# Modulation strips that fill whole quadrants, and a new order of the first chains, in a two-layer diffusion trunk

## The chip, the cores and the metric

The kernel runs on one core of one Trainium2 chip. The metric is the device time of one execution in microseconds, as the median of several runs.

## What is computed

Two layers of a diffusion trunk are applied to 1024 latent tokens and 128 context tokens of width 1024, in float32. Each layer begins with an adaptive modulation: for each of the two conditions, `c` for the latent tokens and `c_ctx` for the context tokens,

```
m = silu(cond) @ w_ada + b_ada            # (1024,) @ (1024, 3072)
shift, scale, gate = split(m, 3)
h = rms_norm(x, norm_g) * (1 + scale) + shift
```

In layer 0 `h @ w_in` feeds a convolution module (two 512-wide halves a and b, gated, a depthwise convolution of width 31, layer norm) and a neighbourhood attention; their outputs are gated, projected and added to x. Layer 1 is a pooling mixer with the same modulation. Products of h and weights are made in three parts: each float32 operand is split into a rounded high half and a low half, and high*high, high*low and low*high are added up in PSUM.

## The kernel before, in words

**Tokens and channels.** The nine token tiles of 128 rows (tile 8 is the context) form three groups of 384: group 0 has tiles 0 to 2, group 1 tiles 3 to 5, group 2 tiles 6 to 8. `norm_x` scales a tile by its rstd: a square with a sum on ScalarE, two small operations on GpSimd, a multiplication on VectorE. `h_chunk(g, ..., k)` makes chunk k (128 channels) of h for a group: three transposes on TensorE into a `tp` bank (there are two), shift and scale on ScalarE, a cast to the high half on VectorE, and the subtraction for the low half, on GpSimd for even k and on VectorE for odd k.

**Modulation of layer 0.** Shift and scale come in four parts m = 0 to 3, each for two chunks of h (2m and 2m + 1), from four loads of 512 KB (`load_wada(m)`). `ada0_rows(m)` is 32 matmuls on TensorE (64 instructions) whose stationary operand is `sc`, silu of the two conditions, two columns for each of eight k. The four strips of a part are put at PSUM partitions 0, 32, 64 and 96, two rows each. Four copies on VectorE (L333) move these rows into `ads`, which a memset has cleared. `ada0_cols(m)` turns `ads` by a transpose (L338) and adds bias and norm weight on VectorE (L273 to L279) to get `SH` and `SC`.

**Modulation of the rest** (gates of both layers, shift and scale of layer 1) is done later in the same manner, a step of 8 matmul instructions at a time between the main chains (`ada_strips`, L360). Two of its strips go through `ada_cols`: a memset of `adr` on GpSimd (L382), four copies on VectorE (L384), then `ada_turn` (L390) transposes.

**The first chains.** `first_chains` runs the first matmuls against w_in: column blocks x = 0 and 1 for group 0 and x = 0 for group 1, six accumulators in PSUM, chunk by chunk as h and weights arrive. `C(k, which)` issues six matmuls (two accumulators, three products) for each pair (x, g) in `which`; `T(k, g)` makes a chunk of h. The weights come in two halves: `split_w0(c, u)` splits the half u (chunks 4u to 4u + 3) of column block c into `whi` on ScalarE (L186) and `wlo` on VectorE (L187). Within `first_chains` TensorE, ScalarE and VectorE take their instructions in the order in which the code is written; GpSimd, SP, and everything after that is ordered by a scheduler. Tiles 6 and 7 are loaded into memory that holds part 3 of w_ada, so their load waits for `ada0_rows(3)`; tile 8 takes the place of tile 0.

**After that** the other column blocks follow on TensorE, while the depthwise convolution goes on beside them: some taps on ScalarE (L551) and GpSimd (L553), the others on VectorE (L564). The copies of `ada_cols` stand in VectorE's queue among those taps.

**Names in the profile.** `wada` is a part of w_ada of layer 0, `wad` a step of the rest, `tp`, `mm` and `cv` are PSUM banks, `whi`/`wlo` the halves of weights, `h` those of h.

Of the kernel before, what the change touches and what calls it, by code (L numbers as in the profile page):

```python
# [15 lines left out]
P = 128  # L16
# [3 lines left out]
G = 384  # L20
# [26 lines left out]
def _body(tc, nc, A, O, const, wp, arena, tmpp, smp, psp):  # L47
# [33 lines left out]
    make_identity(nc, ident)  # L81
    mhalf = const.tile([P, 16], F32, name="mhalf")
    gp.memset(mhalf, -0.5)
# [59 lines left out]
    ve.scalar_tensor_tensor(cu, th0, 1.0, V[:, :16], ALU.add, ALU.mult)  # L143
    sc = const.tile([P, 8, 2], F32, name="sc")
    ve.tensor_scalar(sc.rearrange("p k c -> p c k"), cu.rearrange("p (c k) -> p c k", c=2), 0.5, None, ALU.mult)

# [136 lines left out]
    ads = [const.tile([P, P], F32, name=f"ads{i}") for i in range(2)]  # L283
    for t in ads:
        gp.memset(t, 0.0)
    for t in range(3):
# [19 lines left out]
    raw0[0, 0] = load_raw0(0, 0)  # L306
    raw0[1, 0] = load_raw0(1, 0)
    for t in range(3, 6):
        load_x(t)
    load_wada(1)  # L310
    load_wada(2)
# [3 lines left out]
    for t in (6, 7):  # L315
        load_x(t)
    split_w0(0, 0)
    adb = {}

    def ada0_rows(m):  # L320

        b = adb[m] = bank("tp")
        for k in range(8):
            for x in range(2):
                for q in range(2):
                    r = 32 * (2 * x + q)
                    te.matmul(
                        b[r : r + 2, :P], sc[:, k, :], wt[m, k // 4, x][:, k % 4, q * P : (q + 1) * P],
                        start=(k == 0), stop=(k == 7), tile_position=(0, r),
                    )  # L330
        t = ads[m % 2]
        for r in range(0, P, 32):
            ve.tensor_copy(t[r : r + 2, :], b[r : r + 2, :P])  # L333

# [13 lines left out]
    def ada_strips(l, col, n, fin):  # L348
# [3 lines left out]
        def step(k):  # L352
# [5 lines left out]
            for q in range(4):  # L358
                r = 32 * q
                te.matmul(  # L360
                    st["b"][r : r + 2, :n], sc[:, k, :], w[:, q * n : (q + 1) * n],
                    start=(k == 0), stop=(k == 7), tile_position=(0, r),
                )
# [14 lines left out]
    def ada_cols(l, b, c0):  # L378

        t = slot(ADS[st_i[0] % len(ADS)], name="adr")[:, :G]  # L380
        st_i[0] += 1
        gp.memset(t[:98, :], 0.0)  # L382
        for r in range(0, P, 32):
            ve.tensor_copy(t[r : r + 2, :], b[r : r + 2, :G])  # L384
        return lambda: ada_turn(l, t, c0)
# [79 lines left out]
    def first_chains():  # L465
# [10 lines left out]
        def T(k, g):  # L476
            h_chunk(g, [xt[t] for t in range(3 * g, 3 * g + 3)], 0, h0, k, "tp")

        h0[0] = hslots(range(4))
        ada0_rows(0)  # L480
        ada0_cols(0)
        T(0, 0)
        T(1, 0)
        for k in range(2):
            C(k, ((0, 0),))
        split_w0(1, 0)
        for t in range(3, 6):
            norm_x(t)
        h0[1] = hslots(range(4, 8))
        for k in range(2):  # L490
            C(k, ((1, 0),))
        T(0, 1)
        T(1, 1)
        ada0_rows(1)
        for k in range(2):
            C(k, ((0, 1),))
        ada0_cols(1)
        for k in (2, 3):
            for g in range(2):
                T(k, g)  # L500
        for m in (2, 3):
            ada0_rows(m)
            C(2 * m - 2)
            ada0_cols(m)
            T(2 * m, 0)
            T(2 * m, 1)
            if m == 2:
                split_w0(0, 1)
            C(2 * m - 1, ((0, 0), (1, 0)))
            T(2 * m + 1, 0)  # L510
            T(2 * m + 1, 1)
            if m == 2:
                split_w0(1, 1)
            C(2 * m - 1, ((0, 1),))
        for x in bs:
# [958 lines left out]
```

## Time and profile before

| | |
|---|---|
| median of 3 runs | 974.99 us (974.53 to 975.31) |
| the profiled execution | 977.55 us, span 975.8 us |
| TensorE busy | 948.4 us, 97% of the span |
| VectorE, ScalarE, GpSimd busy | 601.9, 404.4, 369.8 us |
| mean granted TensorE clock | 0.996 |

Times in the profile count from the start of the span. A row of the timeline gives start, duration, engine, line, operation, output and inputs, and how many instructions are merged in it; in brackets stands the idle time ahead of it and the engine or transfer that ended it. PE is TensorE's matmul queue, PEld its weight loads. In rows that merge matmuls the duration holds the pipelined tail of the last one.

### The profile page before, as it was taken

The numbers are of one execution on the slowest core, as the hardware profiler recorded it, in microseconds if no ns is written. First come the engines' busy times: TensorE is split into PE (matmuls) and PEld (weight loads), VectorE is DVE, ScalarE is ACT, GpSimd is POOL, SyncE is SP. The second block draws the span as 40 slices with busy tenths as digits, with TensorE's granted clock in tenths as the row PEclk, the third lists the DMA queues.
The fourth block names the chain that finished last, engine by engine and source line by source line (L and its number), as shares of the span: only waits on it lengthen the run. The fifth ranks groups of instructions, "written<-read, shape, count | busy, mean of one in ns | idle before, by whom it ended". The sixth has DMA issues, their size and how long they took to land.

```text
span 975.8 us, 16659 instructions
## 1 busy us (share of the span) xinstructions
PE 948.4 (97%) x6388; PEld 866.3 (89%) x6388; DVE 601.9 (62%) x1243; ACT 404.4 (41%) x815; POOL 369.8 (38%) x485
## 2 busy tenths in 40 slices
PE   4999999899999999999999999999999999999998
PEld 2899888789999999987887888889999999998887
DVE  3658999989783444457778447666335554585332
ACT  4374676765411244238887223344222122231010
POOL 2354899889943201024456145430000000004231
PEclk9999999899999999999999999999999999999999
DMA  9946955525111111135335412251111111133211
GB/s 311 304 190 153 348 183 184 173 88 185 46 47 46 48 44 44 36 90 142 109 114 175 130 65 108 84 165 44 34 43 33 44 44 55 65 112 129 105 65 66
DMA packets 87531, 108.54 MB, mean 111 GB/s; under 512 B 10700, under 2 KB 73036, under 8 KB 87339
## 3 DMA queue, kind: packets, MB, share of 16 engines
q1 hardware_dynamic: 82539, 95.93, 30.9%
q0 software_dynamic: 2576, 9.18, 2.4%
q10 hardware_dynamic: 2336, 2.36, 0.7%
q8 instruction: 50, 0.82, 0.3%
q14 instruction: 30, 0.25, 0.1%
HBM read 94.64 MB, written 21.57 MB: 119 GB/s over the span
## 4 chain that ended last, share of the span: by engine, by line
PE 82%; POOL 5%; DVE 3%; DMA 3%; ACT 2%; issue 2%; SPq 1%; DVEq 0%; ACTq 0%; POOLq 0%
PE mm L230 33%; PE mm L237 15%; PE mm L1210 10%; PE mm L1203 10%; POOL zc L553 5%; PE cv L985 3%; PE tp L976 2%; PE mm L952 2%; PE mm L1373 2%; DVE cv L564 1%; DMA x<-in_x_sample 1%; DMA raw<-in_w_in 1%; PE tp L443 1%; SPq L212 1%; PE cv L230 1%
## 5 line engine op out<-in xcount | busy, mean ns | idle before, releaser
L230 PE MATMUL mm<-h,whi 128*128 128x384 f32 x1504 | 389.5, 339 | 1.0 <-POOL h L450 0.4
L230 PEld LDWEIGHTS mm<-h,whi 128*128 128x128 f32 x1504 | 271.6, 189 | 6.8 <-issue 2.0
L230 PE MATMUL mm<-h,wlo 128*128 128x384 f32 x752 | 252.8, 337 | 0.0
L553 POOL TENSOR_TENSOR zc<-zc,gr 128x384 f32<-128x384 f32 x138 | 148.5, 1078 | 32.7 <-ACT gr L551 24.5
L237 PE MATMUL mm<-whi,h 128*128 128x256 f32 x864 | 160.6, 287 | 0.0
L237 PEld LDWEIGHTS mm<-whi,h 128*128 128x128 f32 x864 | 137.4, 194 | 6.5 <-ACT vst L694 3.3
L230 PEld LDWEIGHTS mm<-h,wlo 128*128 128x128 f32 x752 | 141.9, 189 | 0.0
L237 PE MATMUL mm<-wlo,h 128*128 128x256 f32 x432 | 123.3, 285 | 0.0
L187 DVE TENSOR_TENSOR wlo<-raw,whi 128x1024 fp32r<-128x1024 f32 (+1 forms) x56 | 67.5, 1206 | 53.3 <-ACT whi L186 53.2
L564 DVE SCALAR_TENSOR_TENSOR cv<-u,convw,cv 128x384 f32<-128x384 f32 (+1 forms) x208 | 95.8, 514 | 1.3
L1210 PE MATMUL mm<-wrh,zs 128*128 128x512 f32 x288 | 92.4, 392 | 0.2 <-POOL wrh L1179 0.2
L1203 PE MATMUL mm<-whi,zs 128*128 128x512 f32 (+1 forms) x304 | 92.5, 379 | 0.0
L186 ACT CAST whi<-raw 128x1024 fp32r<-128x1024 f32 (+1 forms) x56 | 56.9, 1018 | 69.8 <-PE mm L230 25.9
L237 PEld LDWEIGHTS mm<-wlo,h 128*128 128x128 f32 x432 | 84.0, 194 | 0.0
L1217 POOL TENSOR_TENSOR y<-y,og 128x512 f32<-128x512 f32 x34 | 48.6, 1430 | 83.4 <-DVE og L1215 80.3
L551 ACT ACTIVATE gr<-u,convw 128x384 f32<-128x384 f32 (+2 forms) x128 | 64.3, 531 | 30.5 <-POOL zc L553 29.8
L970 POOL TENSOR_SCALAR p<-p,st 128x512 f32<-128x512 f32 x64 | 48.6, 773 | 47.6 <-DVE st L968 31.7
L1203 PEld LDWEIGHTS mm<-whi,zs 128*128 128x128 f32 x304 | 56.0, 188 | 10.6 <-ACT whi L186 0.2
L1210 PEld LDWEIGHTS mm<-wrh,zs 128*128 128x128 f32 x288 | 53.9, 188 | 11.8 <-POOL wrh L1179 0.6
L1215 DVE TENSOR_TENSOR og<-mm,gr 128x512 f32<-128x512 f32 x34 | 23.3, 687 | 59.3 <-PE mm L1210 35.0
L533 ACT ACTIVATE th<-mm 128x384 f32<-128x384 f32 x48 | 23.5, 489 | 81.7 <-PE mm L230 81.5
L1203 PE MATMUL mm<-wlo,zs 128*128 128x512 f32 (+1 forms) x152 | 57.2, 378 | 0.0
(215 smaller groups left out, 1393.2 us busy)
## 6 DMA issues: line engine op xcount, KB each, us to landing
raw<-in_w_in SPq DMA_DIRECT2D x28, 512.0 KB
wad<-in_w_ada SPq DMA_DIRECT2D x16, 768.0 KB
wada<-in_w_ada SPq DMA_DIRECT2D x16, 512.0 KB
raw<-in_w_in SPq DMA_DIRECT2D x32, 256.0 KB
raw<-in_w_out SPq DMA_DIRECT2D x16, 512.0 KB
y0scr<-y POOLq DMA_DIRECT2D x9, 512.0 KB, 3.2
y<-y0scr SPq DMA_DIRECT2D x9, 512.0 KB
x<-in_x_sample SPq DMA_DIRECT2D x8, 512.0 KB
```

What stands on the lines that cost most here:

```text
L186: se.copy(hi[:, :n], raw[:, :n])
L187: ve.tensor_tensor(lo[:, :n], raw[:, :n], f(hi[:, :n]), ALU.subtract)
L230: te.matmul(out, wsl(units, a, k, c0, P), hsl(hs, b, k, g), start=(k == 0 and i == 0), stop=(k == nk - 1 and i == 2))
L237: te.matmul(out, hsl(hs, p, k, g, a, P), wsl(units, q, k, 0, 256), start=(k == 0 and i == 0), stop=(k == 7 and i == 2))
L551: se.activation(pr[:, o : o + n], src, AF.Copy, scale=w)
L553: gp.tensor_tensor(z, z, pr, ALU.add)
L564: ve.scalar_tensor_tensor(zp if k == 30 else acc, src, convw[:, c, k : k + 1], zp if k == NPTS[c] else acc, ALU.mult, ALU.add)
L970: gp.tensor_scalar(ps[i][:, e, :], ps[i][:, e, :], st[:, 4 + e : 5 + e], 0.0, ALU.mult, ALU.add)
L985: te.matmul(ob[64 * e : 64 * e + 64, i * P : (i + 1) * P], vw[j0 + i][x][:, 64 * e : 64 * e + 64], pts[i][:, e, n * P : (n + 1) * P], star ...
L1203: te.matmul(b[:, c0 : c0 + n], zs[p][:, k, :], WL[k // 2][q][:, k % 2, c0 : c0 + n], start=(k == 0 and i == 0), stop=(k == 7 and i == 2))
L1210: te.matmul(b, zs[p][:, k, :], WR[q][k // 3][:, k % 3, :], start=(k == 0 and i == 0), stop=(k == 7 and i == 2))
L1217: gp.tensor_tensor(yv, yv, t, ALU.add)
```

## The change

`sc` becomes a tile of 48 columns, the 16 values in the order of k and zeros behind them, and each strip matmul takes 32 columns of it from column 2k on. A strip then fills all 32 partitions of its quadrant: the first two rows are the two conditions as before, the other thirty hold products that nobody reads. One copy takes the whole bank, and the memsets of `ads` and `adr` go. Part 1 of w_ada is loaded ahead of tiles 3 to 5. The body of `first_chains` is written in another order, and the first split of weights stands behind the first `ada0_cols`.

```
-    sc = const.tile([P, 8, 2], F32, name="sc")
-    ve.tensor_scalar(sc.rearrange("p k c -> p c k"), cu.rearrange("p (c k) -> p c k", c=2), 0.5, None, ALU.mult)
+    sc = const.tile([P, 48], F32, name="sc")
+    gp.memset(sc, 0.0)
+    ve.tensor_scalar(sc[:, :16].rearrange("p (k c) -> p c k", c=2), cu.rearrange("p (c k) -> p c k", c=2), 0.5, None, ALU.mult)
...
-    for t in ads:
-        gp.memset(t, 0.0)
...
+    load_wada(1)
     for t in range(3, 6):
         load_x(t)
-    load_wada(1)
...
-                        b[r : r + 2, :P], sc[:, k, :], wt[m, k // 4, x][:, k % 4, q * P : (q + 1) * P],
+                        b[r : r + 32, :P], sc[:, 2 * k : 2 * k + 32], wt[m, k // 4, x][:, k % 4, q * P : (q + 1) * P],
...
-        t = ads[m % 2]
-        for r in range(0, P, 32):
-            ve.tensor_copy(t[r : r + 2, :], b[r : r + 2, :P])
+        ve.tensor_copy(ads[m % 2], b[:, :P])
...
-                    st["b"][r : r + 2, :n], sc[:, k, :], w[:, q * n : (q + 1) * n],
+                    st["b"][r : r + 32, :n], sc[:, 2 * k : 2 * k + 32], w[:, q * n : (q + 1) * n],
...
-        gp.memset(t[:98, :], 0.0)
-        for r in range(0, P, 32):
-            ve.tensor_copy(t[r : r + 2, :], b[r : r + 2, :G])
+        ve.tensor_copy(t, b[:, :G])
```

The new body of `first_chains`, where `one` is the pairs (0, 0) and (1, 0), `two` the pair (0, 1); beside it, the old one is in the listing above:

```
        ada0_rows(0); ada0_cols(0); split_w0(0, 0)
        T(0, 0); T(1, 0)
        C(0, (0, 0)); C(1, (0, 0)); split_w0(1, 0); C(0, (1, 0)); C(1, (1, 0))
        ada0_rows(1); ada0_cols(1); T(2, 0); T(3, 0)
        norm_x(3); norm_x(4); norm_x(5)
        C(2, one); C(3, one); T(0, 1); T(1, 1)
        ada0_rows(2); C(0, two); ada0_cols(2); T(2, 1); T(3, 1); C(1, two)
        T(4, 0); T(4, 1); split_w0(0, 1); C(2, two)
        T(5, 0); T(5, 1); split_w0(1, 1); C(3, two); C(4, one)
        ada0_rows(3); C(4, two); ada0_cols(3); T(6, 0); T(6, 1)
        C(5, one); T(7, 0); T(7, 1); C(5, two)
```

(Some lines are joined here by semicolons, and loops over k are written out.)

On TensorE, the rows around part 1's turn, the transpose of `ads`, before: it follows matmuls of group 1's chunks 0 and 1 (the accumulators `cv`).

```order
L230 MATMUL cv_248<-h_344,wlo_232 128x384
L230 MATMUL cv_247<-h_344,whi_231 128x384
L230 MATMUL cv_247<-h_345,whi_231 128x384
L230 MATMUL cv_247<-h_344,wlo_232 128x384
L230 MATMUL cv_248<-h_344,whi_231 128x384
L230 MATMUL cv_248<-h_345,whi_231 128x384
L230 MATMUL cv_248<-h_344,wlo_232 128x384
L338 MATMUL tp_376<-ident,ads_146 128x98
L443 MATMUL tp_429<-ident,x_116 128x128
L443 MATMUL tp_429<-ident,x_118 128x128
```

The same place after, from the end of part 1's rows to the first matmul of chunk 2:

```order
L326 MATMUL tp_334<-wada_186,sc 32x128 x2
L326 MATMUL tp_334<-wada_189,sc 32x128 x2
L335 MATMUL tp_334<-ident,ads_147 128x98
L438 MATMUL tp_372<-ident,x_116 128x128
L438 MATMUL tp_372<-ident,x_118 128x128
L438 MATMUL tp_372<-ident,x_120 128x128
L438 MATMUL tp_380<-ident,x_116 128x128
L438 MATMUL tp_380<-ident,x_118 128x128
L438 MATMUL tp_380<-ident,x_120 128x128
L232 MATMUL mm_238<-h_244,whi_286 128x384
```

The twelve matmuls between the rows and the turn are gone from there; group 1's chunks come after part 2's rows.

On ScalarE, the squares of tiles 6 and 7 (`x_227` and `x_229` before) among the chunks 6 and 7 of h, before:

```order
L186 CAST whi_568<-raw_214 128x1024
L126 ACTIVATE gr_73,ss_757<-x_227 128x1024
L448 ACTIVATE h_641<-tp_637,SH_137,SC_139 128x384
L448 ACTIVATE h_649<-tp_645,SH_137,SC_139 128x384
L126 ACTIVATE gr_73,ss_763<-x_229 128x1024
L448 ACTIVATE h_669<-tp_665,SH_137,SC_139 128x384
L448 ACTIVATE h_677<-tp_673,SH_137,SC_139 128x384
```

and after, where the tiles are `x_226` and `x_228`:

```order
L188 CAST whi_558<-raw_213 128x1024
L443 ACTIVATE h_628<-tp_624,SH_138,SC_140 128x384
L443 ACTIVATE h_636<-tp_632,SH_138,SC_140 128x384
L126 ACTIVATE gr_73,ss_744<-x_226 128x1024
L126 ACTIVATE gr_73,ss_750<-x_228 128x1024
L443 ACTIVATE h_656<-tp_652,SH_138,SC_140 128x384
L443 ACTIVATE h_664<-tp_660,SH_138,SC_140 128x384
```

Both squares now stand between chunk 6 and chunk 7.

On VectorE, the copies of the first strip that goes through `ada_cols`, among taps of two convolution accumulators, before:

```order
L564 SCALAR_TENSOR_TENSOR cv_2084<-u_1169,convw,cv_2084 128x384
L384 COPY adr_1927<-tp_1519 2x384
L564 SCALAR_TENSOR_TENSOR cv_1893<-u_743,convw,cv_1893 128x256
L384 COPY adr_1927<-tp_1519 2x384 x3
L564 SCALAR_TENSOR_TENSOR cv_2084<-u_1169,convw,cv_2084 128x384
```

and after:

```order
L570 SCALAR_TENSOR_TENSOR cv_2067<-u_1156,convw,cv_2067 128x384
L570 SCALAR_TENSOR_TENSOR cv_1880<-u_730,convw,cv_1880 128x128
L379 COPY adr_1914<-tp_1506 128x384
L570 SCALAR_TENSOR_TENSOR cv_2067<-u_1156,convw,cv_2067 128x384
L570 SCALAR_TENSOR_TENSOR cv_1880<-u_730,convw,cv_1880 128x256
```

One tap of 384 columns that stood ahead of the copies, and the tap of 256 that stood between them, now stand behind the copy. On TensorE the place of that transpose among the matmuls is unchanged.

More of the change, by code (lines that the diff above doesn't have):

```diff
@@ L81, in _body @@
     make_identity(nc, ident)
-    mhalf = const.tile([P, 16], F32, name="mhalf")
+    mhalf = const.tile([P, 8], F32, name="mhalf")
     gp.memset(mhalf, -0.5)
@@ L316, in _body @@
         load_x(t)
-    split_w0(0, 0)
     adb = {}
@@ L477, in T @@
             h_chunk(g, [xt[t] for t in range(3 * g, 3 * g + 3)], 0, h0, k, "tp")
+        one, two = ((0, 0), (1, 0)), ((0, 1),)
         h0[0] = hslots(range(4))
@@ L481, in first_chains @@
         ada0_cols(0)
+        split_w0(0, 0)
         T(0, 0)
@@ L486, in first_chains @@
         split_w0(1, 0)
+        for k in range(2):
+            C(k, ((1, 0),))
+        ada0_rows(1)
+        ada0_cols(1)
+        T(2, 0)
+        T(3, 0)
         for t in range(3, 6):
@@ L489, in first_chains @@
         h0[1] = hslots(range(4, 8))
-        for k in range(2):
-            C(k, ((1, 0),))
+        C(2, one)
+        C(3, one)
         T(0, 1)
         T(1, 1)
[L494 to L514, printed above, removed]
+        ada0_rows(2)
+        C(0, two)
+        ada0_cols(2)
+        T(2, 1)
+        T(3, 1)
+        C(1, two)
+        T(4, 0)
+        T(4, 1)
+        split_w0(0, 1)
+        C(2, two)
+        T(5, 0)
+        T(5, 1)
+        split_w0(1, 1)
+        C(3, two)
+        C(4, one)
+        ada0_rows(3)
+        C(4, two)
+        ada0_cols(3)
+        T(6, 0)
+        T(6, 1)
+        C(5, one)
+        T(7, 0)
+        T(7, 1)
+        C(5, two)
         for x in bs:
```

## The prediction

> **What bounds the kernel now.** The page comes first, for the span and the busy shares.
>
> ```profile
> span 975.8 us, 16659 instructions
> PE 948.4 (97%) x6388; PEld 866.3 (89%) x6388; DVE 601.9 (62%) x1243; ACT 404.4 (41%) x815; POOL 369.8 (38%) x485
> ```
>
> TensorE is busy for 97%, so a change is worth what it does to TensorE's 27.4 us of idle time, and to the speed at which it runs. The view of windows, cut where TensorE's state changes, says where that time lies (columns: PE, weight loads, DVE, ACT, POOL, then the granted clock).
>
> ```profile
> 0.00:21.31 21.31, 7.49 (x73) 3.81 (x73) 6.66 (x16) 8.09 (x12) 5.58 (x44) 1.00 0.92 306
> 21.31:63.54 42.23, 40.85 (x386) 36.91 (x387) 27.58 (x60) 19.95 (x35) 16.30 (x28) 1.00 0.95 301
> 63.54:170.99 107.45, 107.45 (x729) 96.64 (x727) 96.26 (x193) 71.71 (x140) 82.44 (x80) 1.00 0.62 201
> 170.99:174.14 3.15, 0.00 (x1) 0.03 (x1) 3.06 (x7) 1.78 (x3) 2.96 (x3) 0.84 0.26 86
> 174.14:179.60 5.46, 5.46 (x26) 5.46 (x27) 5.43 (x18) 3.58 (x7) 5.04 (x5) 0.50 0.59 192
> ```
>
> The change touches three of these stretches. Before 21.31 TensorE idles 13.8 us for data. In the first chains (21.31 to 63.54) it idles 1.4 us. Then it never stops until 170.99, where it stands still for 3.15 us and afterwards gets half the clock for 5.46 us. The view of TensorE's waits names the two long ones:
>
> ```profile
> PE tp L327 <- DMA wada<-in_w_ada: 8.1, 3, 6.3
> PE tp L390 <- POOL zc L553: 3.2, 1, 3.2
> ```
>
> The first is the wait for the first part of w_ada, whose loads the change leaves in place. The second is ada_turn's transpose of the strip `adr`. GpSimd is named as releaser, but the vector queue shows who came last:
>
> ```profile
> 168.85 2.57 DVE L564 SCALAR_TENSOR_TENSOR cv<-u,convw,cv 128x128 f32<-128x128 f32 x6
> 171.33 0.54 DVE L384 COPY adr<-tp 2x384 f32<-2x384 f32 x1
> 171.80 0.47 DVE L564 SCALAR_TENSOR_TENSOR cv<-u,convw,cv 128x256 f32<-128x256 f32 x1
> 172.30 1.70 DVE L384 COPY adr<-tp 2x384 f32<-2x384 f32 x3
> 174.14 0.72 PE L390 MATMUL tp<-ident,adr 98*128 98x98 f32 x3 [3.15 <-POOL zc L553]
> ```
>
> The four copies stand in a saturated queue of convolution taps and end at 174.00; the transpose starts 0.14 later.
>
> **The copy of the strips (a gain at 171).** One copy of 128x384 replaces four of 2x384 and a memset. A copy's time goes with its columns, not with its rows: 384 columns on 2 partitions take 0.54, and the next fence has 128 columns on 2 partitions at 1.19 / 4 = 0.30 and 48 columns on 48 partitions at 0.21. So I take 0.54 for the new one and 0.30 for the 128 columns of part copies. By the order, the new copy also stands one 384-column tap (about 0.5) earlier, and the tap between the copies now stands behind it. On the old clock it would end at 171.33 - 0.5 + 0.54 = 171.4 instead of 174.00. TensorE arrives at 170.99 with unchanged work ahead of it, so the wait would be 0.4 + 0.14 = 0.5, if both queues shift alike. The order of the loads on SP for the next weight units changes too (one ahead of two table writes), which may move the vector queue by a microsecond either way; I take a wait of 1.0, with 0 and 3.15 as ends. Gain: 3.15 - 1.0 = 2.15. With the pause that short I let the clock stay up, which returns half of 5.46, 2.73.
>
> **The start of the first chains (a gain at 20).**
>
> ```profile
> 3.46 0.21 DVE L138 COPY V<-tp 128x48 f32<-128x48 f32 x1 [3.46 <-PE tp L137]
> 16.12 1.19 DVE L333 COPY ads<-tp 2x128 f32<-2x128 f32 x4 [4.83 <-PE tp L327]
> 17.34 1.23 DVE L187 TENSOR_TENSOR wlo<-raw,whi 128x1024 fp32r<-128x1024 f32 x1
> 17.45 0.40 PE L338 MATMUL tp<-ident,ads 98*128 98x98 f32 x1 [1.38 <-DVE ads L333]
> 18.59 0.16 DVE L273 TENSOR_TENSOR SH<-tp,V 128x4 f32<-128x4 f32 x1
> 19.82 0.36 DVE L449 CAST h<-h 128x384 fp32r<-128x384 f32 x1 [0.80 <-ACT h L448]
> 20.26 1.00 POOL L450 TENSOR_TENSOR h<-h,h 128x384 fp32r<-128x384 f32 x1 [9.76 <-DMA x<-in_x_sample]
> 21.31 0.69 PE L230 MATMUL mm<-h,whi 128*128 128x384 f32 x1 [0.39 <-POOL h L450]
> ```
>
> Today the shift waits for four copies and for the weight split (1.23) that stands ahead of it. After, one copy ends at 16.4, the transpose at 16.9, shift and scale at about 17.5; the split moves behind them and ends at 18.7, the cast at 19.05, GpSimd's low half at 20.1. The matmuls start 1.2 earlier. The memset of `sc` replaces two larger ones on GpSimd and is hidden by the load of the vectors.
>
> **The new order of the chains (a loss at 27 to 60).** Here the change takes cover away. The rows, by step:
>
> ```profile
> 21.31 6.56 PE mm L230 x23
> 28.96 1.93 PE L327 MATMUL tp<-wada,sc 128*2 128x128 f32 x64 [0.43 <-ACT h L448]
> 30.89 2.29 PE cv L230 x12
> 33.30 0.16 DVE L273 TENSOR_TENSOR SH<-tp,V 128x4 f32<-128x4 f32 x1 [1.01 <-PE tp L338]
> 34.97 1.00 POOL L450 TENSOR_TENSOR h<-h,h 128x384 fp32r<-128x384 f32 x1 [4.58 <-DVE h L449]
> 42.19 2.11 PE mm L230 x12
> 44.30 0.65 PE tp L443 x6
> ```
>
> Part 1: its rows now follow the first 24 matmuls (20.1 + 6.6 = 26.7) and end at 28.6. Today 12 matmuls (2.29) stand between these rows and the turn, and cover the copies. After, the turn follows at once: copy and transpose 0.5, then from the shift to GpSimd's low half 35.97 - 33.30 = 2.7, some 3.3 in all. TensorE has the turn, six transposes (0.65) and one matmul for that time, so it idles about 2.3. Loading part 1 earlier buys nothing here: today these rows wait for ScalarE (the 0.43 above), not for their load.
>
> ```profile
> 21.39 1.05 ACT L126 ACTIVATE gr<-x 128x1024 f32<-128x1024 f32 x1
> 26.86 0.75 DVE L128 TENSOR_SCALAR x<-x,rstd 128x1024 f32<-128x1024 f32 x1 [0.71 <-POOL rstd L114]
> 20.00:30.00 10.00, 8.94 (x70) 8.23 (x74) 5.88 (x9) 6.07 (x10) 5.40 (x8) 1.00 1.09 353
> ```
>
> Group 1's normalisation takes 27.61 - 21.39 = 6.2 from its first square and now starts behind part 1's h, at about 31.4, so it ends at 37.6. TensorE is through with chunks 2 and 3 of group 0 (24 matmuls, 4.2) at 36.2: another 1.0 idle. Its x also lands later, with part 1's 2.1 MB ahead of it: 6 us at 353 GB/s, so by 27.4 if it landed at 21.4 before, well ahead of 31.4. Against these two pauses goes about 1.0 of small waits that stand there today (0.43 is one of them).
>
> ```profile
> 41.26 0.34 PE tp L443 x3
> 47.82 1.22 DVE L187 TENSOR_TENSOR wlo<-raw,whi 128x1024 fp32r<-128x1024 f32 x1
> ```
>
> Chunk 4 needs the second halves of the weights. From its transposes to the end of the second split today's queue takes 49.04 - 41.26 = 7.8, and nothing needs that split until after part 3's rows. After, the second half is used ahead of those rows, behind twelve transposes, 18 matmuls and two more: 1.3 + 3.15 + 0.35 = 4.8. The gap of 3.0 shrinks since transposes wait for their banks too; I take 2.2.
>
> ```profile
> 45.93 1.93 PE L327 MATMUL tp<-wada,sc 128*2 128x128 f32 x64
> 52.58 1.06 ACT L126 ACTIVATE gr<-x 128x1024 f32<-128x1024 f32 x1 [5.68 <-DMA x<-in_x_sample]
> ```
>
> Tiles 6 and 7 load into slots of part 3, so they land 52.58 - 47.86 = 4.7 after its rows. Those rows come later by the moved chains, and by the order both squares now stand ahead of chunk 7's h on ScalarE. That h is ready 4.7 + 2 x 1.2 + 0.6 = 7.7 after the rows, cast and low half 0.4 to 1.7 later (the low half stands behind tile 6's scaling). TensorE needs it after 30 matmuls and twelve transposes, 5.3 + 1.3, and a turn, some 7.0. That is 1.1 idle for the cast and up to 2.4 for the low half, less the little that stands there today; I take 1.1.
>
> Sum of the chains: 2.3 + 1.0 - 1.0 + 2.2 + 1.1 = 5.6 later, less the 1.2 of the start: 4.4. Its ends are 2 (the pauses half as long) and 7 (the unshrunk gaps). Nothing later takes that up, as TensorE does not wait from 63.54 to 170.99, and the vector queue of taps starts behind the same chains.
>
> **Wider weights.** The strips' stationary operand has 32 columns instead of 2.
>
> ```profile
> L327 PEld LDWEIGHTS tp<-wada,sc 128*2 128x2 f32 x256 | 6.9, 91 | 11.7 <-issue 6.7 <-DMA wada<-in_w_ada 2.7 <-ACT h L448 1.2
> L985 PEld LDWEIGHTS cv<-pt,vw 128*64 128x64 f32 x384 | 20.7, 137 | 3.2 <-issue 2.3 <-ACT pt L1139 0.9
> 470.56 1.97 PE L985 MATMUL cv<-pt,vw 128*64 128x128 f32 x32
> ```
>
> From 2 to 64 columns a load grows by 46 ns, so 30 columns cost some 22 ns each, and 448 loads 10 us if all lay on the path. But L985 has the same 128 columns streaming, on two column tiles with 64 columns of weights each: 1.97 / 32 = 62 ns, 123 for a round of its two tiles. L327 needs 1.93 / 64 = 30 ns, 121 for a round of four tiles with 2 columns each. Four loads of 32 columns are as much as two of 64, so a round should take 121 to 123: 2 ns x 16 rounds x 4 parts are 0.13, and with the strips of the other parts 0.2. I take this, the nearest row. The Trainium skill's "TensorE: Matmul & The Clock Gate", section "LDWEIGHTS (loading the stationary operand)", has the time go as the columns over 1.2 GHz, which would make the sum about 11 us worse if nothing hid it; the trace agrees on the slope and shows it hidden.
>
> **The sum.** 4.4 + 0.2 - 2.15 - 2.73 = -0.3. The profiled execution took 977.55 for its span of 975.8; the median of the plain runs is 974.99, 2.56 less. So 977.25 for such an execution, and 974.7 for the median. What measurement can tell from no change is 0.2%, 1.95 us: faster ends at 973.0, slower begins at 976.9.
>
> **Rivals.** (1) The forecast: the loss in the chains and the gain at 171 cancel, 974.7, by themselves 973.0 to 976.9; chance 0.47. (2) The clock falls in the new pauses. In the window of the old wait the granted clock averages 0.84, so it was halved in the last 2 x 0.16 x 3.15 = 1.0, after some 2.1 of idling. The wait for the split weights (2.2 to 3.0) and part 1's pause (2.3, broken by transposes) reach that point. Each fall costs up to 2.73: 977.4 for one, 980.2 for both. For it: the only long pause of the trace ended so. Against: theirs are just at the bound and hold transposes. Chance 0.18. The Trainium skill's page "TensorE: Matmul & The Clock Gate", section "Part 1: The HAM clock gate (the \"warmup\" mystery)", asks for an idle window of about 3.4 us; by that rule these pauses keep the clock, and the trace shows the fall sooner. (3) The wait at 171 stays, because the taps fall further behind than TensorE; from a lag of 2 us more the clock falls again: 974.99 + 4.6 = 979.6; chance 0.10. (4) Weight loads lie on the path: 10 us more, 984.7; chance 0.03. (5) The pauses of the chains are half as long, the split weights and tile 7 arriving in time: 2.0 in place of 4.4, and no wait at 171: 974.99 + 2.0 + 0.2 - 3.15 - 2.73 = 971.3. For it: the vector engine sheds 12 part copies in this stretch. Against: each pause is a chain of rows and no queue. Chance 0.22.
>
> **Range and chances.** Faster 0.22, same 0.47, slower 0.18 + 0.10 + 0.03 = 0.31. The range runs from case 5 to case 3 with both ends' neighbours, 971.3 to 979.6, and leaves out case 4, the double fall of case 2, and tails.
>
> **What would show it.** In the profile after, TensorE's idle time between 20 and 68 should be near 7 us, with waits before the first matmul of chunk 2 (about 2), before a matmul on the second split's low half (about 2) and before chunk 7; the first chains should end near 68 in place of 63.5. The transposes of `adr` should wait 1 us or less, with the clock at 1.00 behind them. Strip rounds should keep 1.9 for 64 matmuls. I am wrong if the first chains end by 65 (the covers I missed), if the clock drops ahead of 60, or if the wait at `adr` is still over 2.

## The result, and the profile after

| | before | after |
|---|---|---|
| median of 4 runs each | 975.15 us (974.53 to 976.22) | 983.90 us (981.19 to 984.62) |
| ratio, 95% interval | | 1.0083 [1.0064, 1.0103] |
| the profiled execution, its span | 977.55, 975.8 | 981.19, 979.4 |

The kernel is slower by 8.75 us, outside the range that the prediction gave. The two profiled executions differ by only 3.6 us, since that of before lies 2.40 above its median and that of after 2.71 below its own: 3.64 + 2.40 + 2.71 = 8.75. So the profile shows where the loss sits, and the medians how large it usually is. Part of the reason shows in the trace of after: its first 24 matmuls take 4.2 us (19.89 to 24.07) where those of before take 6.4 (21.31 to 27.71), most of them at twice the duration. None of the other 19 profiled executions has its first matmuls at that speed. Not even that of f1 below has, whose code is the same up to the first transpose of `adr`; its part 3's strips begin 1.6 us later than in after. So this profile flatters the kernel after.

The page of after, its first lines:

```profile
span 979.4 us, 16631 instructions
PE 948.1 (97%) x6388; PEld 867.6 (89%) x6388; DVE 596.2 (61%) x1225; ACT 403.9 (41%) x815; POOL 370.6 (38%) x482
```

VectorE is busy for 5.7 us less than before, as the change meant, and TensorE as long as before; what grew is TensorE's idle time. The view of windows, cut at the events of before (first full matmul chain, first chains done, TensorE stops for `adr`; the second only roughly, since the order of the matmuls there is another):

```profile
0.00:19.89 19.89, 7.18 (x74) 4.63 (x74) 5.96 (x13) 8.25 (x12) 5.43 (x43) 1.00 0.93 291
19.89:69.41 49.52, 42.89 (x389) 38.11 (x390) 24.30 (x51) 19.94 (x34) 15.81 (x27) 0.93 0.86 278
69.41:175.96 106.55, 106.55 (x725) 97.06 (x724) 95.20 (x186) 69.51 (x136) 80.92 (x77) 1.00 0.62 199
175.96:182.00 6.04, 2.97 (x16) 2.97 (x16) 6.04 (x14) 3.80 (x7) 5.57 (x7) 0.72 0.37 99
```

The chains start 21.31 - 19.89 = 1.4 us earlier. They idle 49.52 - 42.89 = 6.6 us where they idled 1.4, at a clock of 0.93 instead of 1.00, and end at 69.41 instead of 63.54. From there TensorE runs without a stop to 175.96, and stops at `adr` as before. The waits by name that the change brought or kept:

```profile
PE tp L385 <- DVE adr L379: 3.1, 1, 3.1
PE mm L232 <- DVE wlo L189: 2.6, 2, 2.4
PE mm L232 <- DVE h L444: 1.4, 2, 0.7
PE mm L232 <- POOL h L445: 1.3, 2, 0.6
PE tp L335 <- DVE ads L330: 0.8, 2, 0.4
```

And TensorE's timeline at the places of which the prediction spoke:

```profile
26.44 0.30 PE L335 MATMUL tp<-ident,ads 98*128 98x98 f32 x1 [0.41 <-DVE ads L330]
...
28.41 0.45 PE L232 MATMUL mm<-h,whi 128*128 128x384 f32 x1 [0.74 <-DVE h L444]
...
29.49 0.45 PE L232 MATMUL mm<-h,whi 128*128 128x384 f32 x1 [0.64 <-POOL h L445]
...
35.53 1.96 PE L326 MATMUL tp<-wada,sc 128*32 128x128 f32 x64 [0.43 <-ACT h L443]
...
48.53 0.44 PE L232 MATMUL mm<-h,wlo 128*128 128x384 f32 x1 [2.36 <-DVE wlo L189]
...
49.86 3.11 PE L326 MATMUL tp<-wada,sc 128*32 128x128 f32 x64
...
60.57 0.26 PE L174 MATMUL tp<-ident,rows 54*128 54x54 f32 x1 [0.46 <-ACT h L443]
...
62.26 0.49 PE L232 MATMUL mm<-h,whi 128*128 128x384 f32 x1 [0.49 <-DVE h L445]
...
62.86 0.84 PE L232 MATMUL mm<-h,whi 128*128 128x384 f32 x2
...
65.74 0.60 PE L232 MATMUL mm<-h,whi 128*128 128x384 f32 x2
...
179.03 0.75 PE L385 MATMUL tp<-ident,adr 98*128 98x98 f32 x3 [3.07 <-DVE adr L379]
```

Two things stand there beside the pauses. Part 3's strips (49.86) take 3.11 us where the same 64 matmuls took 1.96 at 35.53: behind the wait ahead of them the granted clock was 0.58 on average (48.80 to 52.90). From 62.26 to 65.74 it was 0.54, and two matmuls take 0.84 where they took 0.51 before the waits of 0.46 and 0.49. And the strips of part 3 begin at 49.86, not at 45.93, with what hangs on them. ScalarE and VectorE of after, the square of tile 6, the split of the fourth half of weights of the next column blocks, the tap ahead of the copy of `adr`, and that copy:

```profile
57.62 1.06 ACT L126 ACTIVATE gr<-x 128x1024 f32<-128x1024 f32 x1 [1.48 <-DMA x<-in_x_sample]
...
104.32 1.05 ACT L188 CAST whi<-raw 128x1024 fp32r<-128x1024 f32 x1 [4.61 <-DMA raw<-in_w_in]
...
105.40 1.23 DVE L189 TENSOR_TENSOR wlo<-raw,whi 128x1024 fp32r<-128x1024 f32 x1 [3.30 <-ACT whi L188]
...
175.21 1.36 DVE L570 SCALAR_TENSOR_TENSOR cv<-u,convw,zc 128x384 f32<-128x384 f32 x1 [0.42 <-POOL zc L559]
...
178.43 0.55 DVE L379 COPY adr<-tp 128x384 f32<-128x384 f32 x1
```

Of before, the rows that answer to the split and to the tap (the square was at 52.58, the last copies at 172.30 + 1.70):

```profile
99.64 1.22 DVE L187 TENSOR_TENSOR wlo<-raw,whi 128x1024 fp32r<-128x1024 f32 x1 [0.95 <-ACT whi L186]
...
167.57 1.36 DVE L564 SCALAR_TENSOR_TENSOR cv<-u,convw,zc 128x384 f32<-128x384 f32 x1 [0.40 <-POOL zc L553]
```

The square is 5.0 us later, the split 5.8, and the tap, which in both kernels has just waited 0.4 for GpSimd (`zc` is the accumulator of GpSimd's taps), 7.64. From the tap to the end of the copying it is 178.98 - 175.21 = 3.77 us instead of 174.00 - 167.57 = 6.43, so the single copy and its earlier place are worth 2.66. TensorE arrives 4.97 later (175.96 for 170.99). VectorE is later than TensorE by 7.64 - 4.97 = 2.67 at the tap, the copy saves just that, and the wait at `adr` is what it was.

### The profile page after: what moved, and what is told of

Same layout as the page of the kernel before. It is cut to its first block, busy times and chain, and to the rows that moved or that the text cites. A ratio compares the mean times of both kernels' runs of the same rounds, so it can differ in the third digit from the quotient of the medians.

```text
span 979.4 us, 16631 instructions
## 1 busy us (share of the span) xinstructions
PE 948.1 (97%) x6388; PEld 867.6 (89%) x6388; DVE 596.2 (61%) x1225; ACT 403.9 (41%) x815; POOL 370.6 (38%) x482
## 3 DMA queue, kind: packets, MB, share of 16 engines
q10 hardware_dynamic: 2336, 2.36, 0.7%
## 4 chain that ended last, share of the span: by engine, by line
PE 80%; DVE 8%; DMA 5%; SPq 2%; issue 2%; ACT 2%; POOL 1%; DVEq 0%; ACTq 0%; POOLq 0%
PE mm L232 32%; PE mm L239 14%; PE mm L1216 10%; PE mm L1209 10%; DVE cv L570 5%; PE cv L991 3%; DMA wada<-in_w_ada 2%; PE tp L982 2%; PE mm L958 2%; PE mm L1379 2%; DMA raw<-in_w_in 1%; POOL zc L559 1%; SPq L214 1%; DVE wlo L189 1%; DMA raw<-in_w_out 1%
## 5 line engine op out<-in xcount | busy, mean ns | idle before, releaser
L559 POOL TENSOR_TENSOR zc<-zc,gr 128x384 f32<-128x384 f32 x138 | 150.8, 1094 | 31.9 <-ACT gr L557 23.3
L189 DVE TENSOR_TENSOR wlo<-raw,whi 128x1024 fp32r<-128x1024 f32 (+1 forms) x56 | 67.9, 1214 | 49.8 <-ACT whi L188 49.1
```

What stands on the lines that cost most here:

```text
L189: ve.tensor_tensor(lo[:, :n], raw[:, :n], f(hi[:, :n]), ALU.subtract)
L559: gp.tensor_tensor(z, z, pr, ALU.add)
```

## The experiments

Eighteen kernels, each timed beside the kernel before on the same chip. In the first four, theory A is that the new order of chains and loads makes the loss, B that the full quadrants do. In the next four, A is narrower (TensorE's pauses are the loss, each worth its length). Theory E, formed from those, is that part 3's strips come late, tile 6 is loaded behind them, and ScalarE and VectorE run late from there.

**e1_strips.** The kernel before with the full quadrants alone: `sc` of 48 columns, 32-column strips, one copy each, no memsets (and a constant, `mhalf`, of 8 columns for 16, as in after).

> The kernel before with the full-quadrant strips alone; loads, chains and the first split stay as they were. Theory A (the new order of the chains is the loss): the one copy ends 2.6 us earlier on the vector queue, the transpose of adr waits 1 us or less instead of 3.15, the clock stays up behind it (2.7 us), and the first matmuls start 0.9 us earlier: about 969.5, at most 972. Theory B (the wide strips are the loss, by weight loads or by the products that nobody reads): slower than before, up to the 983.9 of the whole change, and a round of 64 strip matmuls takes clearly more than 1.93 us.

976.29 us, ratio 1.0016 [1.0001, 1.003]. Neither theory holds: no gain, and no loss near 8 us. The wait at `adr` fell to 1.91, not to 1.

**e2_order.** The kernel before with the new loads, the new place of the first split and the new chains, strips and copies as they were.

> The kernel before with the new loads, the new place of the first split and the new order of the chains; strips of two rows with four copies. Theory A: as slow as the whole change or slower, 983 to 987, since the strips take nothing from the chains; the first chains end near 69 instead of 63.5 and the transpose of adr waits 3 us or more. Theory B: near 975, as before.

986.66 us, 1.0109 [1.0089, 1.0129]: the order makes the whole loss. With the full quadrants it is some 2.5 less (1.0109 to 1.0083), but the intervals overlap, so that they soften it is not shown. Its waits show by what:

```profile
PE tp L389 <- DVE adr L383: 4.9, 1, 4.9
PE tp L337 <- DVE ads L332: 2.9, 3, 1.4
PE mm L230 <- DVE wlo L187: 2.6, 2, 2.4
```

The three waits for `ads` are 2.9 us with four copies each and 0.8 with one (after, above): where a turn has no matmuls to cover it, these waits are 2 us shorter with the single copy.

**e3_turn.** The kernel before with one line more, `adq[17], adq[18] = adq[18], adq[17]`: the first `adr` transpose comes one strip step later.

> The kernel before, with the transpose of the first adr strip moved one step of the strips later (the first step of the next strip takes its place). If that wait costs what the trace of before says, 3.15 us of standing still and 2.7 us of halved clock, this takes 969.3. Rival: the pause only moves to another place or its clock is lost there: 975, no change.

972.79 us, 0.9988 [0.997, 1.0005]. Its profiled span is 970.7, which is 5.1 less than that of before (a wait of 3.15 and half a clock's 5.46 gone), but its median is only 1.9 less. The kernel before ran between 972.6 and 977.7 in these comparisons; the profiled execution, with 977.55, is at the upper end. The wait and the clock's fall as the profile had them were not there to be won in every run. Single executions also differ ahead of the edit: the split of e3 begins at 98.19, 1.45 earlier than that of before, though the edit acts only at 171.

**e4_strips_split.** e1 with the first split behind part 0's turn, as in after.

> As e1, with the first split of weights written behind part 0's turn too. By the working of the prediction the first full matmul then starts 1.2 us earlier than before, of which the copies alone give a part; the time is 0.3 to 1.0 us under e1. Rival: the start is lost again behind a later wait or in the clock's warm-up: the same as e1 within 0.5 us.

976.19 us, 1.0012 [0.9995, 1.0028]. The first full chain starts at 20.04 (1.3 earlier than before), yet the square of tile 6 starts at 52.79 against 52.58: the start's gain is gone by then.

**f1_after_turn.** The kernel after with e3's line.

> The kernel after, with the first strip's transpose (adr) taken one strip step later. Theory A (the 8.7 us are the sum of pauses that TensorE shows, each worth its own length): the wait of 3.07 us at adr and some 1.5 us of half clock behind it go, so 983.9 - 4.6 = about 979.3. Rival B (the wait only marks how far VectorE's taps are behind, and the next thing that TensorE needs of VectorE is as late): the wait reappears behind another instruction before 200 us, and the time stays within 982.5 to 984.5. The same edit on the kernel before took 1.9 us off a wait of 3.15 us, which would make 982.0 here, between the two.

985.11 us, 1.01 [1.0082, 1.0118]: no gain. The first strip's transposes now stand at 181.97 and wait for nothing. But the second strip's, which waited for nothing in after, now wait 4.24 for their copy:

```profile
225.46 0.75 PE L385 MATMUL tp<-ident,adr 98*128 98x98 f32 x3 [4.24 <-DVE adr L379]
225.92 0.56 PE L239 MATMUL mm<-whi,h 128*128 128x256 f32 x1
```

B is right on the mechanism (VectorE is behind, and the next thing that TensorE needs of it is late), wrong on the place: it came at 225, not ahead of 200. Behind the wait matmuls of this shape take 0.41 us and more, where they take 0.28 at 185, so the clock fell there too.

**f3_late_c4.** The kernel after with chunk 4's first chains behind part 3's strips:

```
-        C(4, one)
         ada0_rows(3)
+        C(4, one)
         C(4, two)
```

> The kernel after, with chunk 4's three chains for the first group of accumulators put behind part 3's rows instead of ahead of them. Theory A (pauses sum up): the 2.36 us wait for the second split's low half shrinks to 0.4 us or less, since the 1.96 us of part 3's strips stand in it, and the strips run at full clock again (1.96 instead of 3.11 us), so the first chains end about 3.1 us earlier, at 66.3, and the time is 983.9 - 3.1 = 980.8. Rival C (the loads of tiles 6 and 7 set when the first chains can end, whatever TensorE does before them): the wait goes but TensorE then waits for h of chunk 7 by as much, and the time is 983 to 984.

977.21 us, 1.0022 [1.0007, 1.0036]: from 1.0083 to 1.0022 are 6 us back, twice what the pause and the clock behind it come to ((2.36 - 0.32) + (3.11 - 1.96) = 3.2). TensorE's strips, and the square of tile 6 on ScalarE:

```profile
45.93 1.29 PE L326 MATMUL tp<-wada,sc 128*32 128x128 f32 x36
...
50.42 0.45 PE L232 MATMUL mm<-h,wlo 128*128 128x384 f32 x1 [0.32 <-DVE wlo L189]
```

```profile
53.39 1.06 ACT L126 ACTIVATE gr<-x 128x1024 f32<-128x1024 f32 x1 [6.18 <-DMA x<-in_x_sample]
```

The strips begin where they did before the change, the wait of 2.36 is 0.32, and tile 6 is there 4.2 us sooner than in after. This one line carries nearly three quarters of the loss. It takes away the pause, the fall of the clock and the late tile together, so it does not tell what each costs.

**g5_cover.** The kernel after with twelve matmuls (half of the 24 of which the expectation speaks) back between part 1's strips and its turn: `ada0_rows(1)` ahead of `C(0, ((1, 0),))` and `C(1, ((1, 0),))`.

> The kernel after, with the 24 matmuls of chunks 0 and 1 for the second slice put between part 1's strips and their transpose, as chains stood there before. Theory A: the waits of 0.41, 0.74 and 0.64 us at part 1's transpose and its chunk 2 fall to about 0.4 together, so 983.9 - 1.4 = 982.5, if part 1's weights have landed by 22 us; if they have not, a new wait at the strips takes up to 2 us and nothing is won. Rival C (the loads of tiles 6 and 7 set the end of the first chains): 983.5 to 984.5, the gain reappearing as a longer wait for the second split's low half or for h of chunk 7.

983.20 us, 1.0079 [1.0063, 1.0095]. Between the two expectations and within the spread of after: inconclusive. Of part 1's waits the one for `ads` went, those for h stayed.

**f2_loads.** The kernel before with `load_wada(1)` ahead of tiles 3 to 5 and nothing else.

> The kernel before, with only the loads of part 1's weights put ahead of those of tiles 3 to 5; its chains, splits and strips as before. Theory A (the order of the chains is the loss): part 1's strips wait for nothing in the kernel before, so the time stays at 974.7, within 1 us. Rival D (the new order of the loads is itself a loss, because tiles 3 to 5 land later and group 1's first h with them): TensorE shows a new wait of 2 us or more ahead of the chains of chunk 0 and 1 of group 1, and the time is 977 or more.

980.74 us, 1.0049 [1.003, 1.0069]: D, and dearer than it said.

```profile
28.41 0.31 PE L443 MATMUL tp<-ident,x 128*128 128x128 f32 x1 [0.46 <-DVE x L128]
...
29.80 0.33 PE L443 MATMUL tp<-ident,x 128*128 128x128 f32 x1 [1.08 <-DVE x L128]
...
31.78 0.66 PE L443 MATMUL tp<-ident,x 128*128 128x128 f32 x4 [1.65 <-DVE x L128]
32.87 3.51 PE L327 MATMUL tp<-wada,sc 128*2 128x128 f32 x64 [0.43 <-ACT h L448]
...
51.45 1.93 PE L327 MATMUL tp<-wada,sc 128*2 128x128 f32 x64
```

Three waits for late tiles, 3.2 together, then strips at half clock (3.51), and part 3's strips at 51.45 instead of 45.93. Tile 6's square follows at 58.50. That is the pattern of after, got by another cause.

**h1, h2, h3, h4.** Four kernels cut the tie between part 3's strips and tile 6: parts 2 and 3 swap two memory slots, so that tiles 6 and 7 go where part 2 was. h1 is after, h2 before, h3 is f3 and h4 is e3 with this line:

```
-    WAS = (0, 1, 4, 5, 2, 3, 6, 7, 8, 9, 10, 11, 16, 21, 22, 23)
+    WAS = (0, 1, 4, 5, 2, 3, 6, 7, 16, 9, 10, 23, 8, 21, 22, 11)
```

> The kernel after, with one table changed: part 3's weights take two slots of part 2's and the other way round, so that the loads of tiles 6 and 7 follow part 2's strips (done near 37.5 us) and no longer part 3's (begun at 49.9 us). Chains, strips and the order of the loads stay. Theory E (part 3's strips stand behind chunk 4's chains and their wait, tiles 6 and 7 are loaded behind them, and ScalarE and VectorE are late from there on): the load of tile 6 is issued near 45.2 us instead of 51.8, its square starts near 52.6 instead of 57.6, the waits of chunk 7 go, the wait at adr falls from 3.07 to under 1, while the 2.36 us wait for the second split stays; the time is 978 to 980. Theory A (TensorE's own pauses are the loss): the loads change nothing, 983 to 984.5.

> The kernel before with the same table changed and nothing else. Theory E: the load of tile 6 is issued at 45 instead of 47.0 us; if the queue of loads lets it land as much earlier, VectorE gains up to 2 us, the wait of 3.15 us at adr falls to about 1.5 and the time is 973. Rival: the loads keep the DMA engines full until then, tile 6 lands within 0.5 us of 52.6 and the time stays at 974.7, within 0.7.

> The kernel after, with both mends: chunk 4's chains of the first group behind part 3's strips (977.2 us by itself) and the table of the slots changed. Theory E: tile 6's load is issued at 45.2 instead of 47.0 us, 1 to 2 us less, 975.5 to 976.5. If tile 6's landing is bound by the bytes loaded ahead of it, 977.2 stays.

> The kernel before with the table of the slots changed and the first strip's transpose (adr) one strip step later, the edit that took 1.9 us by itself. If the two gains add up: 971.5. If tile 6's landing is bound by the bytes ahead of it, the turn's gain alone: 973.

992.75, 982.30, 987.99 and 980.49 us; ratios 1.0176 [1.0156, 1.0195], 1.0081 [1.0067, 1.0095], 1.0139 [1.012, 1.0159], 1.0057 [1.0041, 1.0072]. All were slower by 7 to 11 us than the same kernel without the line, which no expectation held. ScalarE, VectorE and TensorE of h2:

```profile
52.45 1.06 ACT L126 ACTIVATE gr<-x 128x1024 f32<-128x1024 f32 x1 [5.83 <-DMA x<-in_x_sample]
```

```profile
54.54 0.75 DVE L128 TENSOR_SCALAR x<-x,rstd 128x1024 f32<-128x1024 f32 x1 [4.67 <-POOL rstd L114]
56.02 0.75 DVE L128 TENSOR_SCALAR x<-x,rstd 128x1024 f32<-128x1024 f32 x1 [0.72 <-POOL rstd L114]
...
56.86 0.15 DVE L278 TENSOR_TENSOR SC<-tp,V 128x4 f32<-128x4 f32 x1
```

```profile
57.16 0.87 PE L443 MATMUL tp<-ident,x 128*128 128x128 f32 x3 [5.41 <-DVE SC L278]
```

The load of tile 6 is issued 1.2 us earlier (45.85 for 47.01) but lands when it did: its square starts at 52.45 for 52.58. And since the tie is gone, the scheduler puts the scaling of tiles 6 and 7 ahead of part 3's shift and scale on VectorE (54.54 and 56.02 ahead of 56.86); VectorE takes them in that order, so TensorE waits 5.41 us for a shift and scale that stand behind the tiles' landing. In h1 the square stands ahead of an h on ScalarE and TensorE waits 9.99 us for that. So these runs say that tile 6 does not land before about 52, and that the order of the queues hangs on the slots; they do not test E.

**j1_x6_twice.** The kernel before with tile 6 loaded twice:

```
     for t in (6, 7):
         load_x(t)
+        if t == 6:
+            sy.dma_start(xt[t], x_src(t))
```

> The kernel before with one line more: tile 6 is loaded twice, the second load into the same place behind the first. No instruction of TensorE, VectorE or GpSimd is added or moved by hand. Theory E (when tile 6 lands sets how late ScalarE and VectorE run from 52 us on, and that comes back as waits of TensorE): the square of tile 6 starts 3 to 5 us later than 52.6, the first tap 3 to 5 us later than 74.3, the wait of 3.15 us at adr grows by 2 to 4 us, and the time is 978 to 980. Theory A (TensorE's pauses ahead of 60 us are the loss, tile 6 only follows them): there are none here, so the time stays at 974.7 to 975.7.

978.91 us, 1.0037 [1.0022, 1.0051]: E. A late tile 6 costs about 4 us with TensorE's order of work untouched, so A does not hold as the only cause; that pauses cost too is not excluded. ScalarE's square, then TensorE's new waits:

```profile
57.00 1.06 ACT L126 ACTIVATE gr<-x 128x1024 f32<-128x1024 f32 x1 [3.10 <-DMA x<-in_x_sample]
```

```profile
58.76 0.26 PE L172 MATMUL tp<-ident,rows 54*128 54x54 f32 x1 [0.91 <-ACT h L450]
...
60.45 0.69 PE L230 MATMUL mm<-h,whi 128*128 128x384 f32 x1 [0.49 <-DVE h L452]
...
61.25 0.84 PE L230 MATMUL mm<-h,whi 128*128 128x384 f32 x2
...
178.40 0.44 PE L392 MATMUL tp<-ident,adr 98*128 98x98 f32 x3 [3.82 <-DVE adr L386]
```

The square is 4.4 us late, TensorE waits for chunk 7's h, the clock halves for the next matmuls (0.84), and the wait at `adr` is 3.82. (This profiled execution began 1.0 us late, with its first full chain at 22.32 instead of 21.31, so 3.4 of the 4.4 are the second load. Its own 512 KB did not hold up the loads behind it for long: those of `vwin` are issued from 57.95 instead of 57.00, no later than the execution itself. The weights of the later splits are issued 2.8 to 3.7 later.)

**g7_old_loads.** The kernel after with the loads as before.

> The kernel after with the loads in the order of before (tiles 3 to 5 ahead of part 1's weights), its chains and strips as they are. By the run of the kernel before with the new loads alone (980.7, 5 us slower) the new load order would be a loss of its own: without it tiles 3 to 5 land earlier, the 0.46 us wait for x goes, and the time falls to 980 to 982. Rival: the new order of the chains needs part 1's weights by 24 us, so TensorE waits 2 to 4 us for them at part 1's strips, everything behind moves by as much, part 3's strips too, and the time is 985 to 988.

985.02 us, 1.0104 [1.0078, 1.013]: the rival. TensorE waits 0.21 and 1.11 for part 1's weights, its strips end later, part 3's begin at 54.32, tile 6's square at 61.94. The new load order is a loss for the old chains and, if anything, a help to the new ones.

**k1_adr, k2_adr_turn.** The kernel before with the full quadrants for the later strips only; k2 has e3's line too.

> The kernel before with the full quadrants for the later strips (adr) alone; the four parts at the start keep two rows and four copies, and so ScalarE's order ahead of 80 us stays that of before. If the full quadrants cost what they did at the start only because they moved ScalarE's first taps 3 us later: the copies at adr take 0.55 instead of 2.25 us, the wait of 3.15 us falls to about 1.4, the time is 972.5 to 973.5. Rival: VectorE gains nothing at the first strip, since what it waits for there is GpSimd (zc), and the time stays at 974.7, within 0.7.

> The same with the first strip's transpose one strip step later, which took 1.9 us by itself: the wait at adr is gone altogether, no clock falls there, and the time is 971 to 972.5 in every run, with less spread than before's 972.6 to 977.6. Rival as for the kernel before this one: 972.8, what the later transpose gives alone.

975.27 and 975.21 us, 1.0002 [0.999, 1.0014] and 1.0001 [0.9989, 1.0014]. The rival's time for k1; k2 gained nothing over it. VectorE and TensorE of k1:

```profile
100.33 1.23 DVE L188 TENSOR_TENSOR wlo<-raw,whi 128x1024 fp32r<-128x1024 f32 x1 [1.23 <-ACT whi L187]
...
169.63 1.36 DVE L563 SCALAR_TENSOR_TENSOR cv<-u,convw,zc 128x384 f32<-128x384 f32 x1 [0.42 <-POOL zc L552]
...
173.78 0.54 DVE L383 COPY adr<-tp 128x384 f32<-128x384 f32 x1
...
174.38 0.75 PE L389 MATMUL tp<-ident,adr 98*128 98x98 f32 x3 [2.61 <-DVE adr L383]
```

From the split to the end of the copy it is 174.32 - 100.33 = 73.99 us; before it was 174.00 - 99.64 = 74.36. The single copy does save its 1.7: from the tap to the end of the copying it is 4.69 instead of 6.43. But from the split to the tap VectorE takes 69.30 instead of 67.93, and that eats 1.4 of it. The rows between show by what. Four multiplications of the gates, on 2x256 values, take 1.72 + 1.31 = 3.03 us on VectorE, where before they took 0.68 + 0.28 + 0.66 = 1.62. ScalarE then waits 1.84 for VectorE at 140.19, GpSimd 1.85 for ScalarE at 141.74, and the last long run of GpSimd's taps begins at 152.43 instead of 150.42; the tap on VectorE waits for one of these, as the rival has it. Why the same four multiplications take longer was not tested.

**m1_turn_split, m2_late_turn.** e3 with the first split behind part 0's turn; f3 with e3's line.

> The kernel before with the first strip's transpose (adr) one strip step later (972.8 by itself) and the first split of the input weights behind part 0's transpose, as in the kernel after. If the start's gain of 1.1 us reached the end, 971.7; if the landing of tile 6 near 52.6, bound by the bytes ahead of it, takes it back, 972.8 again and TensorE waits about 1 us longer ahead of 60 us.

> The kernel after with two mends: chunk 4's chains of the first group behind part 3's strips (977.2 by itself) and the first strip's transpose one strip step later. Its wait at adr was 1.1 us already, so about 1 us less: 976. If VectorE's later first tap (77.9 instead of 74.3) shows up behind another wait instead, 977.2 stays.

973.19 us, 0.9982 [0.9972, 0.9992], and 978.89 us, 1.0042 [1.0025, 1.0058]. m1 is faster than both kernels, than before by 0.18%; it can't be told from e3. Of the change it has only the new place of the first split. m2 gains nothing over f3 and stays behind before.

**All runs beside each other.** Times of the profiled executions: part 3's strips and the square of tile 6 begin, the fourth split of the next weights begins on VectorE, the tap ahead of the copies begins, the copies of the first `adr` end; then the median.

| kernel | strips 3 | square | split | tap | `adr` copied | median |
|---|---|---|---|---|---|---|
| m1 | 45.33 | 52.12 | 98.16 | 166.06 | 172.47 | 973.2 |
| before | 45.93 | 52.58 | 99.64 | 167.57 | 174.00 | 974.3 to 975.4 |
| k1 | 45.83 | 53.00 | 100.33 | 169.63 | 174.32 | 975.3 |
| e1 | 45.50 | 52.67 | 100.79 | 170.54 | 174.32 | 976.3 |
| f3 | 45.93 | 53.39 | 100.23 | 170.03 | 173.81 | 977.2 |
| j1 | 46.74 | 57.00 | 102.78 | 171.70 | 178.25 | 978.9 |
| f2 | 51.45 | 58.50 | 104.71 | 172.70 | 179.14 | 980.7 |
| after | 49.86 | 57.62 | 105.40 | 175.21 | 178.98 | 983.9 |
| f1 | 51.43 | 58.60 | 104.63 | 174.48 | 178.26 | 985.1 |
| e2 | 55.29 | 63.25 | 109.46 | 179.33 | 184.54 | 986.7 |

Where the strips stand late, so does the square, except in j1, where the square alone is late and the rest follows it. The split follows the square by 46 to 48 us. From the split to the tap it is 67.9 to 68.9 us in the kernels with the old strips and the old chains (m1, before, j1, f2), and 69.3 to 69.9 in all others. From the tap to the end of the copying it is 3.8 to 4.7 us with one copy and 5.2 to 6.6 with four. So what the single copy saves behind the tap is for the greater part lost ahead of it, and e1 and k1 gained nothing.

## Why the prediction was wrong

**What held.** The chains start earlier by 1.4 (1.2 forecast). The pauses came where they were put: 0.41 + 0.74 + 0.64 = 1.8 at part 1 (2.3), 0.46 for a tile of group 1 (1.0), 2.36 + 0.26 at the second split (2.2), 0.46 + 0.49 at chunk 7 (1.1), and 6.6 us of idling in the stretch (near 7). The wide weights cost nothing to speak of: 1.96 for 64 matmuls against 1.93, though a load took 135 ns on average in place of 91, twice the growth of 22 that was worked out. The copy of 128x384 took 0.55 (0.54), and with its earlier place it saved 2.66 behind the tap (2.6). The row from which the prediction took "48 columns on 48 partitions" has 128 partitions and 48 columns, which bears its rule out all the more.

**The step that failed: the gain at 171.** The sum took off 2.15 for the wait at `adr` and 2.73 for its clock, and it took both on the condition that "both queues shift alike". They did not. TensorE came 4.97 later to the place, VectorE 7.64 later to the tap ahead of the copies. The 2.67 between them used up the 2.66 that the copy saved. The wait measured 3.07 in place of 1.0, so 2.07 of the 2.15 were missing. The clock fell again (0.50 from 179.03 to 181.90), but for some 3 us and not for 5.46, so of the 2.73 about 1.2 came and 1.5 were missing. The prediction had this as its rival 3, with a chance of 0.10, and two of the three signs that it named for being wrong came: the clock ahead of 60, and a wait at `adr` over 2. Where VectorE's lateness comes from:

- 5.76 us of the 7.64 are there at the split. The prediction had the tie between part 3's strips and tile 6, priced it at chunk 7 only (1.1), and then wrote that the vector queue of taps "starts behind the same chains". j1 shows the other price: with tile 6 late, the split is 3.1 later, the tap 4.1 and the copies 4.3, for 3.6 us by the ratio and 4.7 by the medians, with TensorE's program unchanged. That after's lateness comes the same way is the reading that the table supports; no run holds back tile 6 alone in after.
- 1.88 us more come between the split and the tap (69.81 for 67.93). The four multiplications of the gates make up 1.06 of them (2.68 for 1.62 us); the rest was not taken apart, and why they are longer stays open.

**The second step: the clock.** The forecast let the clock stay up in the new pauses, with 0.18 for the rival that it falls. It fell twice ahead of 66 us: 3.11 - 1.96 = 1.15 in part 3's strips, and about 10 matmuls at 0.32 instead of 0.17 behind chunk 7's waits, 1.5. That the 4.97 by which TensorE is late at 171 lies so near to the forecast 4.6 (4.4 for the chains, 0.2 for the weights) is luck: these two falls cost some 2.65, and the early full speed of this one execution gave back 1.6 of it by part 3's strips (49.86; 51.43 in f1), since the working had taken 6.6 for matmuls that took 4.2. Rivals 2 and 3 came true together; each had been priced alone. The Trainium skill's "TensorE: Matmul & The Clock Gate", section "Part 1: The HAM clock gate (the \"warmup\" mystery)", says that the window in which activity is measured runs freely, so that the point of change depends on where the work falls in it. The runs agree with that: in j1 a wait of 3.82 us was followed by 1.5 us at full clock before it fell to 0.50, in k1 a wait of 2.61 by 0.50 at once. That it takes an idle window of about 3.4 us, as its table has it, they do not show: 2.36 us did it. So the 2.1 us of idling, which the prediction read off one wait as the point of the fall, is no fixed threshold either.

**The base.** The sum was made against a profiled execution at the upper end of the kernel's runs. e3 took its long wait away and gained 5.1 us in the profile, 1.9 in the median and 1.2 by the ratio. Of the 95 runs of before that were timed beside these kernels, the 31 under 974 us show a mean granted clock of 0.999 or 1.000 and the 24 from 976 us on 0.996 to 0.998; the profiled one has 0.996. A stretch of 5.46 us at half clock lowers the mean by 0.5 x 5.46 / 975.8 = 0.003, so the 59 runs with 0.999 or more cannot have had it. A gain read from such a profile should have been discounted before it was set against a loss that every run has.

**Where the loss comes from**, then: `C(4, one)` ahead of part 3's strips (by f3, 0.61 of the 0.83%). It costs a wait for a split that is not ready, the clock behind it, and the landing of tile 6; the shares of the three were not measured apart. The other 2 us were not settled. Full quadrants in the old order cost 1.6 us or less by the medians (e1, e4, k1), and f3 has them too.

## What to carry to other kernels

When instructions are moved, look up what memory they free and which load waits for it: that load's consumer on another engine can be the dearest thing that moves, and it shows far behind the place of the edit. A gain that rests on one queue being shorter holds only if that queue is no later than the engine that waits for it: compare how late each of the two will be at the last instruction ahead of those that are spared. And before a wait in a profile is counted as a gain, see whether the profiled run lies at the upper end of the runs.

## What the runs showed of the hardware

- A load issued earlier need not land earlier: tile 6 was issued at 45.85 instead of 47.01 (h2) and landed within 0.13 us of before, and at 45.58 in h1, with its square at 52.74 (before: 52.58).
- Two waits of half a microsecond, 1.2 us apart, were followed by some 3.5 us at a clock of 0.54 (after, 62.26 to 65.74).
- The length of a wait alone did not say when the clock falls: behind 3.82 us (j1) it stayed up for 1.5 us more, behind 2.61 us (k1) it was 0.50 at once.
- The same four VectorE multiplications on 2x256 values took 1.62 us in before and 3.03 in k1; by what was not found.
- The kernel before ran from 972.6 to 977.7 us without any change. Kernels without its long wait did too (e3: six of ten runs at 972.1 to 972.9, two near 977). In before the granted clock goes with it (0.999 and more under 974 us, 0.998 and less from 976 us on); what makes the clock fall in one run and not in another was not found.
